# At each seam between two stages, two of eight input blocks are multiplied early, as an old and a new term

## The chip, the cores and the metric

The kernel runs on one core of a Trainium2 chip. The metric is the device time of one execution in microseconds (us), the median of several runs; lower is better.

## The reference

A stream of 272 tokens (16 meta tokens and 256 of the sequence) with 1024 features goes through two layers, and its last 256 tokens through a third. Every layer is a chain of stages of one form, "multiply the normed stream by weights, norm the result, add it to the stream":

```python
for i in range(DEPTH):
    g = norm_g[i]
    f1 = swiglu(rmsnorm(h, g[0]), ffn_w_gate[i, 0], ffn_w_up[i, 0], ffn_w_down[i, 0])
    h = h + FFN_RES * rmsnorm(f1, g[1])
    hn = rmsnorm(h, g[2])
    m = neighborhood_attention(hn, ...) if i % N_MIXERS == 0 else diff_attention(hn, ...)
    h = h + rmsnorm(m, g[3])
    f2 = swiglu(rmsnorm(h, g[4]), ffn_w_gate[i, 1], ffn_w_up[i, 1], ffn_w_down[i, 1])
    h = h + FFN_RES * rmsnorm(f2, g[5])
...
x = x + rms_norm(mixed @ w_out, g_mix_post)      # hybrid layer: its input is rms_norm(x, g_mix_pre) @ w_in
u = jnp.square(jax.nn.relu(rms_norm(x, g_mlp_pre) @ w_up))
x = x + rms_norm(u @ w_down, g_mlp_post)
```

`rmsnorm(x, g)` is `x * rsqrt(mean(x*x) + 1e-6) * g`, the mean over the 1024 features of a token. All of it is float32.

## The kernel before

**Layout.** The stream `h` lies transposed in SBUF: eight blocks of 128 features (the partitions), each 272 tokens wide (256 once the meta tokens are no longer needed). A product is a matmul with a 128x128 piece of weight as the stationary operand and one block of the input as the moving one, summed over the eight input blocks in one PSUM tile. There are six such PSUM tiles (`ps_mm`, 128 x 272 each) and two small ones (`ps_t`).

**Precision.** Each float32 operand is split in two float32r parts, a high one and the rest, and three products are summed: high x high, high x low, low x high. For the input these parts are the tiles `xh` and `xl`, for the weights `wh` and `wl`. Weights arrive by DMA, ACT makes `wh` (line 156), DVE makes `wl` (line 168), and up to seven pairs are held; `W.pump` hands out this work between the products.

**A seam.** There are seven places where one stage ends and the next begins, here called seams: after a down projection of a feed-forward stage (four times; three of them 272 columns wide, the fourth, ahead of the hybrid layer, 256 wide), and after an output projection of attention (three times; 272, 256 and 256 columns wide). At a seam this happens:

1. `Post.evac(ps, j)` takes the eight output blocks of the ending stage as they are finished: ACT squares a block (line 387, or 385 in two halves for the last), DVE adds the square to `accf` (line 388), and ACT writes the block times its gain into `f` (line 603). For the last block, PE first sums `accf` over the partitions ("row sums", line 344), then the squares `sq` of the last block.
2. `Post.finish`: DVE makes the mean of both sums (lines 356, 362), POOL raises it to -1/2 (line 349), and PE spreads the result over the partitions in a PSUM tile, `post.bc` (lines 368 to 373). Meanwhile PE runs nine matmuls whose result nobody reads (`turn_over`, line 476), and nine more behind the spreading.
3. DVE makes `f*bc` (`addend`, line 617, tile `hb`), and from it for blocks 0 and 1 the new `xh` at once (line 486); for blocks 2 to 7 it adds `hb` to `h` (line 623) and ACT makes `xh` (line 436). PE starts on each block as its `xh` comes: four output tiles, `wh` and `wl`, that is eight matmuls for each block (lines 502, 503), 64 in all. DVE then makes the eight `xl` (line 453), and PE does 32 matmuls with these (line 506).
4. The norm of the new stream is not in `xh`: it is a factor for each token, `rb`, which is applied to the products. Its squares are made by ACT (line 495) and summed by DVE in three additions, the last of them into `accp` (lines 447 to 449, `Norm.sum`). `Norm.head` makes PE's row sums of `accp` a part of the next product (the fifth output tile): it stands behind that tile's twelfth matmul. `Norm.tail` spreads `rb`.

The order on each engine is the order of the program text; the tile framework sets the semaphores between engines, and it also lets no two engines touch one PSUM tile at the same time.

Of the kernel before, what the change touches and what calls it, by code (L numbers as in the profile page):

```python
# [10 lines left out]
F32 = mybir.dt.float32  # L11
# [10 lines left out]
T = S + NM  # L22
# [13 lines left out]
R_BUFS = 3  # L36

# [172 lines left out]
def block_kernel(ctx: ExitStack, tc: tile.TileContext, a, out):  # L210
# [13 lines left out]
    def nm(s):  # L224
        uid[0] += 1
        return f"{s}_{uid[0]}"
# [196 lines left out]
    class Norm:  # L423


        def __init__(self, g, cols):
            self.g, self.cols = g, cols
            self.xh = bp.tile([128, 8, T], FR, name=nm("xh"), tag="xh", bufs=1)
            self.xl = bp.tile([128, 8, T], FR, name=nm("xl"), tag="xl", bufs=1)
            self.x = (self.xh, self.xl)  # L430
            self.acc = tp.tile([128, T], F32, name=nm("accp"), tag="acc", bufs=1)
            self.first, self.second = {3: self.head}, {1: self.tail}
# [5 lines left out]
        def square(self, j):  # L438
            c = self.cols
            q = square_into(self.acc, h[:, j, c], j, c, engine=pool)  # L440
            if q is not None:
                pool.tensor_tensor(self.acc[:, c], self.acc[:, c], q[:, c], op=OP.add)

        def sum(self, sq):

            c = self.cols
            dve.tensor_tensor(sq[:, 0:4, c], sq[:, 0:4, c], sq[:, 4:8, c], op=OP.add)
            dve.tensor_tensor(sq[:, 0:2, c], sq[:, 0:2, c], sq[:, 2:4, c], op=OP.add)
            dve.tensor_tensor(self.acc[:, c], sq[:, 0, c], sq[:, 1, c], op=OP.add)

# [14 lines left out]
    def start_phase(norm, post, n=4):  # L465
# [22 lines left out]
        for k in range(2, 8):  # L488
# [5 lines left out]
        for x, y in ((2, 6), (6, 8), (0, 2)):  # L494
            act.activation(squares[:, x:y, c], h[:, x:y, c], AF.Square)
            if x:
                W.high()
        for k in range(8):
            norm.low(k)
        for k in range(8):  # L500
            for q in range(n):
                pe.matmul(ps[q][:, c], w[q][0][:, k, :], norm.xh[:, k, c], start=k == 0, stop=False)  # L502
                pe.matmul(ps[q][:, c], w[q][1][:, k, :], norm.xh[:, k, c], start=False, stop=False)  # L503
        for k in range(8):
            for q in range(n):
                pe.matmul(ps[q][:, c], w[q][0][:, k, :], norm.xl[:, k, c], start=False, stop=k == 7)  # L506
        W.low_if()
        norm.sum(squares)
        W.done(n)
        return ps  # L510
# [78 lines left out]
    class Post:  # L589


        def __init__(self, g, cols, bias=None, gbias=None):
            self.g, self.cols, self.bias, self.gbias = g, cols, bias, gbias
# [15 lines left out]
        def finish(self, between=lambda n: None):  # L609
            r = rstd_head(self.m, self.cols, self.sq)  # L610
            between(9)
            self.bc = rstd_tail(r, self.cols)
# [279 lines left out]
    post = Post(half_gains(0, 1), ALL)  # L892
# [42 lines left out]
    norm = Norm(gains(0, 2), ALL)  # L935
# [218 lines left out]
    post = Post(gains(0, 3), ALL, vgain("b_o"), gbo)  # L1154
# [3 lines left out]
    norm = Norm(gains(0, 4), ALL)  # L1158
    post2 = Post(half_gains(0, 5), ALL)
# [14 lines left out]
    norm = Norm(gains(1, 0), ALL)  # L1174
    post = Post(half_gains(1, 1), ALL)
# [3 lines left out]
    norm = Norm(gains(1, 2), ALL)  # L1179
# [115 lines left out]
    post = Post(gains(1, 3), GRID)  # L1295
    proj_out(post, (Oh, Ol))

    norm = Norm(gains(1, 4), GRID)
    post2 = Post(half_gains(1, 5), GRID)
# [3 lines left out]
    norm = Norm(vgain("mix_pre"), GRID)  # L1303
# [17 lines left out]
    pg, *ps4 = start_phase(norm, post2)  # L1321
# [275 lines left out]
    post = Post(vgain("mix_post"), GRID)  # L1597
# [3 lines left out]
    norm = Norm(vgain("mlp_pre"), GRID)  # L1601
# [120 lines left out]
```

## Time and profile before

| | |
|---|---|
| median of 3 runs | 1429.81 us (1429.76 to 1431.71) |
| the profiled execution | 1431.22 us |
| its span, first to last instruction | 1429.4 us |
| mean granted TensorE clock | 0.998 |
| PE busy | 1408.2 us, 99% of the span |
| DVE busy | 893.7 us, 63% |
| ACT busy | 750.2 us, 52% |

A share of busy time is a mean over the whole span; at a seam the engines stand otherwise. Times in the trace are microseconds from the start of the span. PE's weight loads have rows of their own (PEld) and run ahead of the matmul that they belong to.

### The profile page before, as it was taken

How to read it: one execution, taken by the hardware profiler on the slowest of the kernel's cores; microseconds unless marked ns; L12 is line 12 of the kernel's file. 1: busy time of each engine (PE TensorE's matmuls, PEld its weight loads, DVE VectorE, ACT ScalarE, POOL GpSimd, SP SyncE). 2: the span in 40 equal slices, each digit the busy share in tenths (PEclk: the TensorE clock that was granted, in tenths of full speed). 3: DMA queues.
4: the chain of work that ended last, by engine and by line, in shares of the span. 5: the costliest groups of instructions: out<-in, count | busy, mean ns of one | idle time of the engine just before them, and what ended most of it. 6: DMA issues, size and time to landing. Idle time of an engine off the chain costs nothing.

```text
span 1429.4 us, 26895 instructions
## 1 busy us (share of the span) xinstructions
PE 1408.2 (99%) x11068; PEld 1357.6 (95%) x11068; DVE 893.7 (63%) x1668; ACT 750.2 (52%) x1333; POOL 168.1 (12%) x185
## 2 busy tenths in 40 slices
PE   9999999999999999999999999999999999999997
PEld 9999999899999999999999888999999888899886
DVE  6776447664865544955546785776555877686542
ACT  5554346666554444644445564664444565676441
POOL 1325001010221200212100001031100000000000
PEclk9999999999999999999999999999999999999999
DMA  7875552352575554555553352375554543275650
GB/s 250 271 251 172 179 185 66 124 167 90 167 229 172 168 180 148 175 180 177 163 182 99 119 177 89 112 244 184 188 178 131 177 129 108 89 234 179 221 177 30
DMA packets 219528, 234.41 MB, mean 164 GB/s; under 512 B 5313, under 2 KB 209894, under 8 KB 219214
## 3 DMA queue, kind: packets, MB, share of 16 engines
q1 hardware_dynamic: 218206, 227.38, 49.2%
q0 software_dynamic: 656, 4.94, 1.1%
q8 instruction: 87, 1.43, 0.4%
q10 hardware_dynamic: 544, 0.38, 0.1%
q14 instruction: 35, 0.29, 0.1%
HBM read 231.62 MB, written 5.13 MB: 166 GB/s over the span
## 4 chain that ended last, share of the span: by engine, by line
PE 91%; DVE 6%; ACT 2%; DMA 1%; issue 1%; POOL 0%; DVEq 0%; POOLq 0%; ACTq 0%; SPq 0%
PE pm L393 24%; PE pm L395 24%; PE pm L394 23%; PE ps L1645 2%; PE ps L1644 2%; PE ps L1646 2%; PE pm L506 2%; DVE wl L168 2%; PE pm L502 2%; PE pm L503 1%; DMA wr<-in_da_w_qkv_dram 1%; PE pt L344 1%; PE pt L1013 1%; PE pm L540 1%; PE ps L1022 1%
## 5 line engine op out<-in xcount | busy, mean ns | idle before, releaser
L168 DVE TENSOR_TENSOR wl<-wr,wh 128x1024 fp32r<-128x1024 f32 (+1 forms) x430 | 514.3, 1204 | 122.9 <-ACT wh L156 122.2
L393 PE MATMUL pm<-xh,wh 128*128 128x272 f32 (+1 forms) x1992 | 581.4, 292 | 2.2 <-DVE Ol L421 2.2
L395 PE MATMUL pm<-xh,wl 128*128 128x272 f32 (+1 forms) x1992 | 570.4, 286 | 0.0
L394 PE MATMUL pm<-xl,wh 128*128 128x272 f32 (+1 forms) x1992 | 568.5, 285 | 0.0
L156 ACT ACTIVATE wh<-wr 128x1024 fp32r<-128x1024 f32 (+1 forms) x430 | 440.7, 1033 | 194.0 <-PE pm L394 112.9
L393 PEld LDWEIGHTS pm<-xh,wh 128*128 128x128 f32 x1992 | 376.0, 189 | 11.2 <-issue 9.4
L395 PEld LDWEIGHTS pm<-xh,wl 128*128 128x128 f32 x1992 | 375.9, 189 | 0.1
L394 PEld LDWEIGHTS pm<-xl,wh 128*128 128x128 f32 x1992 | 375.6, 189 | 0.1
L395 PE MATMUL pm<-mh,wl 128*128 128x272 f32 (+1 forms) x704 | 202.2, 287 | 0.0
L393 PE MATMUL pm<-mh,wh 128*128 128x272 f32 (+1 forms) x704 | 202.1, 287 | 0.0
L394 PE MATMUL pm<-ml,wh 128*128 128x272 f32 (+1 forms) x704 | 201.5, 286 | 0.0
L650 POOL TENSOR_TENSOR sr<-sl,rb 128x272 f32<-128x272 f32 (+1 forms) x88 | 104.5, 1192 | 320.1 <-ACT sl L648 320.1
L395 PEld LDWEIGHTS pm<-mh,wl 128*128 128x128 f32 x704 | 132.7, 188 | 0.0
L394 PEld LDWEIGHTS pm<-ml,wh 128*128 128x128 f32 x704 | 132.6, 188 | 0.0
L393 PEld LDWEIGHTS pm<-mh,wh 128*128 128x128 f32 x704 | 132.6, 188 | 0.0
L420 ACT ACTIVATE mh<-m 128x272 fp32r<-128x272 f32 (+1 forms) x88 | 37.7, 428 | 117.8 <-DVE m L655 117.6
L655 DVE TENSOR_TENSOR m<-pm,sr 128x272 f32<-128x272 f32 (+1 forms) x88 | 38.3, 435 | 80.5 <-PE pm L395 74.8
L648 ACT ACTIVATE sl<-gq 128x272 f32<-128x272 f32 (+1 forms) x88 | 36.9, 427 | 95.8 <-DVE gq L646 95.6
L349 POOL TENSOR_TENSOR s<-s,mhalf 128x3 f32<-128x3 f32 (+1 forms) x15 | 19.1, 1274 | 558.4 <-DVE s L362 336.1
L646 DVE TENSOR_TENSOR gq<-pm,rb 128x272 f32<-128x272 f32 (+1 forms) x88 | 37.6, 435 | 71.6 <-PE pm L395 69.0
L388 DVE TENSOR_TENSOR accf<-accf,sq 128x272 f32<-128x272 f32 (+1 forms) x42 | 18.3, 436 | 81.9 <-ACT sq L387 81.8
L502 PE MATMUL pm<-xh,wh 128*128 128x272 f32 (+1 forms) x224 | 56.7, 291 | 0.6
(337 smaller groups left out, 1728.6 us busy)
## 6 DMA issues: line engine op xcount, KB each, us to landing
wr<-in_ffn_w_gate_dram SPq DMA_DIRECT2D x43, 1024.0 KB
wr<-in_ffn_w_up_dram SPq DMA_DIRECT2D x43, 1024.0 KB
wr<-in_ffn_w_down_dram SPq DMA_DIRECT2D x32, 1024.0 KB
wr<-in_w_up_dram SPq DMA_DIRECT2D x16, 1024.0 KB
wr<-in_w_down_dram SPq DMA_DIRECT2D x16, 1024.0 KB
wr<-in_ffn_w_down_dram SPq DMA_DIRECT2D x16, 768.0 KB
wr<-in_na_w_qkv_dram SPq DMA_DIRECT2D x12, 1024.0 KB
wr<-in_da_w_qkv_dram SPq DMA_DIRECT2D x12, 1024.0 KB
```

Source lines behind the costliest of these rows:

```text
L156: self.nc.scalar.activation(hi, w, AF.Copy)
L168: engine.tensor_tensor(lo, w, hi.bitcast(F32), op=OP.subtract)
L393: pe.matmul(ps, wh[:, k, :], xh[:, j, cols], start=start, stop=False)
L394: pe.matmul(ps, wh[:, k, :], xl[:, j, cols], start=False, stop=False)
L395: pe.matmul(ps, wl[:, k, :], xh[:, j, cols], start=False, stop=stop)
L420: act.activation(hi, src, AF.Copy)
L502: pe.matmul(ps[q][:, c], w[q][0][:, k, :], norm.xh[:, k, c], start=k == 0, stop=False)
L506: pe.matmul(ps[q][:, c], w[q][0][:, k, :], norm.xl[:, k, c], start=False, stop=k == 7)
L646: dve.tensor_tensor(t[:, c], ps[:, c], norm.rb[:, c], op=OP.mult)
L648: act.activation(s[:, c], t[:, c], AF.Silu)
L650: pool.tensor_tensor(s2[:, c], s[:, c], norm.rb[:, c], op=OP.mult)
L655: dve.tensor_tensor(t[:, c], ps[:, c], gated.pop(f)[:, c], op=OP.mult)
```

## The change

For input blocks 2 and 3 and two of the four first output tiles, the new stream `h + f*bc` is no longer waited for. While the ending stage is still finishing, `Norm.ahead` (called in `evac` for output blocks 5 and 6) splits `g*h` and `g*f` of these two blocks into high and low parts, in places 4 to 7 of `xh` and `xl`, which are free at that time. `start_phase` multiplies both with the weights: 12 matmuls with the old stream go into the output tiles themselves, 12 with `f` into two further PSUM tiles, `term`. These 24 take the place of the 18 matmuls of `turn_over`. When `bc` is there, ACT copies it into SBUF, DVE makes `term*bc` (tile `fs`) between the fourth and the fifth `xl`, and when the tile is complete DVE adds both into an SBUF tile `fb`, from which the next step reads. The 12 matmuls of these blocks and tiles in the main loops are gone, and blocks 2 and 3 come last there.

The core of the diff:

```diff
+AHEAD = (2, 3)
+ORDER = (0, 1, 4, 5, 6, 7, 2, 3)
...
+        def ahead(self, i, f):
+            c, j = self.cols, AHEAD[i]
+            for n, src in ((4 + i, h), (6 + i, f)):
+                act.activation(self.xh[:, n, c], src[:, j, c], AF.Copy, scale=self.g[:, j:j + 1])
+                dve.scalar_tensor_tensor(self.xl[:, n, c], src[:, j, c], self.g[:, j:j + 1],
+                                         self.xh[:, n, c].bitcast(F32), op0=OP.mult, op1=OP.subtract)
...
-        def turn_over(m):
-            x = w[0][0].rearrange("p a b -> p (a b)")[:, 0:256]
+        term = {q: ps_mm() for q in early}
+
+        def products():
+            for x, into in ((4, {q: ps[q] for q in early}), (6, term)):
+                for i in range(2):
+                    k = AHEAD[i]
+                    for q in early:
+                        for part, v in ((0, norm.xh), (1, norm.xh), (0, norm.xl)):
+                            last = x == 6 and i == 1 and part == 0 and v is norm.xl
+                            pe.matmul(into[q][:, c], w[q][part][:, k, :], v[:, x + i, c],
+                                      start=i == 0 and part == 0 and v is norm.xh, stop=last)
+                            yield
+        todo = products()
+        def some(m):
             for _ in range(m):
-                pe.matmul(ps[0][:, 0:256], x[:, 0:128], x, start=True, stop=True)
-
+                next(todo, None)
+        some(3)
         old = [tmp("go") for _ in range(2)]
         for k in range(2):
             act.activation(old[k][:, c], h[:, k, c], AF.Copy, scale=norm.g[:, k:k + 1])
-        post.finish(turn_over)
-        turn_over(9)
+        post.finish(lambda: some(11 if c is ALL else 10))
+        some(24)
+        bc = tmp("bc")
+        act.activation(bc[:, c], post.bc[:, c], AF.Copy)
...
+        scaled = {}
+        for i, k in enumerate(ORDER):
+            norm.low(k)
+            if i == 3:
+                for q in early:
+                    scaled[q] = tmp("fs")
+                    dve.tensor_tensor(scaled[q][:, c], term[q][:, c], bc[:, c], op=OP.mult)
...
         W.low_if()
         norm.sum(squares)
+        for q in early:
+            x = tmp("fb")
+            dve.tensor_tensor(x[:, c], scaled[q][:, c], ps[q][:, c], op=OP.add)
+            ps[q] = x
...
         def evac(self, ps, j):
             c = self.cols
+            if j == 4:
+                self.norm = Norm(self.gain, c)
+            if j in (5, 6):
+                self.norm.ahead(j - 5, self.f)
             if j == NB - 1:
                 self.m = mean_head(self.acc, c)
```

Three places show what this does to the order on the engines. On PE, at the first seam, behind the last matmul of the down projection, stood the row sums of `accf` and of `sq` (tiles `pt`), the nine idle-filling matmuls, and the spreading of the factor `s` with `ident`:

```order
L344 MATMUL pt_2563<-ones,accf_126 128x1 x3
L344 MATMUL pt_2588<-ones,sq_2569 128x1 x3
L476 MATMUL pm_2580<-wh_2402 128x256 x9
L368 MATMUL pt_2605<-ident,s_2594 128x128
L369 MATMUL pt_2605<-ident,s_2594 128x128
L370 MATMUL pt_2605<-ident,s_2594 128x16
```

Now three early products stand between the two groups of row sums, and eleven behind them:

```order
L346 MATMUL pt_2573<-ones,accf_125 128x1 x3
L487 MATMUL pm_2587<-xh_2369,wh_2408 128x272
L487 MATMUL pm_2587<-xh_2369,wl_2409 128x272
L487 MATMUL pm_2587<-xl_2370,wh_2408 128x272
L346 MATMUL pt_2600<-ones,sq_2579 128x1 x3
L487 MATMUL pm_2588<-xh_2369,wh_2438 128x272
L487 MATMUL pm_2588<-xh_2369,wl_2439 128x272
L487 MATMUL pm_2588<-xl_2370,wh_2438 128x272
```

On DVE, at the same seam, the mean (`s`) and the first `hb`, which reads `post.bc` (`pt`), stood like this, with the engine that each waits for:

```order
L356 TENSOR_SCALAR s_2564<-pt_2563 128x3 [waits PE_49]
L362 SCALAR_TENSOR_TENSOR s_2589<-pt_2588,s_2564 128x3 [waits DVE_49,PE_49]
L617 TENSOR_TENSOR hb_2618<-f_125,pt_2605 128x272 [waits PE_49]
L486 SCALAR_TENSOR_TENSOR xh_2573<-hb_2618,G,go_2584 128x272 [waits DVE_49,Activation_49]
L617 TENSOR_TENSOR hb_2621<-f_125,pt_2605 128x272
```

Now the first `hb` waits for ACT (`Activation`), whose one instruction at this place that touches the same PSUM tile is the copy of `bc`:

```order
L358 TENSOR_SCALAR s_2574<-pt_2573 128x3 [waits PE_49]
L364 SCALAR_TENSOR_TENSOR s_2601<-pt_2600,s_2574 128x3 [waits DVE_49,PE_49]
L655 TENSOR_TENSOR hb_2635<-f_124,pt_2619 128x272 [waits Activation_49]
L508 SCALAR_TENSOR_TENSOR xh_2369<-hb_2635,G,go_2596 128x272 [waits DVE_49]
L655 TENSOR_TENSOR hb_2638<-f_124,pt_2619 128x272
```

On DVE, ahead of the seam behind the first output projection, the last three additions of squares into `accf` (output blocks 4, 5 and 6) stood between pairs of weight splits:

```order
L388 TENSOR_TENSOR accf_4123<-accf_4123,sq_4354 128x272
L168 TENSOR_TENSOR wl_4324<-wr_3953,wh_4323 128x1024
L168 TENSOR_TENSOR wl_4327<-wr_3953,wh_4326 128x1024
L388 TENSOR_TENSOR accf_4123<-accf_4123,sq_4393 128x272
L168 TENSOR_TENSOR wl_4360<-wr_4110,wh_4359 128x1024
L168 TENSOR_TENSOR wl_4366<-wr_4110,wh_4365 128x1024
L388 TENSOR_TENSOR accf_4123<-accf_4123,sq_4429 128x272
L356 TENSOR_SCALAR s_4459<-pt_4458 128x3
```

Now two `xl` of `ahead` stand ahead of the second and two ahead of the third of these additions:

```order
L390 TENSOR_TENSOR accf_4137<-accf_4137,sq_4370 128x272
L170 TENSOR_TENSOR wl_4338<-wr_3967,wh_4337 128x1024
L170 TENSOR_TENSOR wl_4341<-wr_3967,wh_4340 128x1024
L453 SCALAR_TENSOR_TENSOR xl_4369<-h,G,xh_4368 128x272
L453 SCALAR_TENSOR_TENSOR xl_4369<-f_4136,G,xh_4368 128x272
L390 TENSOR_TENSOR accf_4137<-accf_4137,sq_4413 128x272
L170 TENSOR_TENSOR wl_4376<-wr_4124,wh_4375 128x1024
L170 TENSOR_TENSOR wl_4382<-wr_4124,wh_4381 128x1024
L453 SCALAR_TENSOR_TENSOR xl_4369<-h,G,xh_4368 128x272
L453 SCALAR_TENSOR_TENSOR xl_4369<-f_4136,G,xh_4368 128x272
L390 TENSOR_TENSOR accf_4137<-accf_4137,sq_4453 128x272
L358 TENSOR_SCALAR s_4483<-pt_4482 128x3
```

## Rows read from the trace of the kernel before

**Rows 1.** The page: busy time and share of the span by engine.

```profile
PE 1408.2 (99%) x11068; PEld 1357.6 (95%) x11068; DVE 893.7 (63%) x1668; ACT 750.2 (52%) x1333; POOL 168.1 (12%) x185
```

**Rows 2.** Timeline, first seam, 272 columns: start, length, engine, line, operation, count.

```profile
213.93 0.76 PEld L344 LDWEIGHTS pt<-ones,accf 128*128 128x128 f32 x6
214.61 0.75 PEld L344 LDWEIGHTS pt<-ones,sq 128*128 128x128 f32 x6
216.66 0.13 PEld L368 LDWEIGHTS pt<-ident,s 128*128 128x128 f32 x1 [0.24 <-POOL s L349]
...
217.26 0.44 DVE L617 TENSOR_TENSOR hb<-f,pt 128x272 f32<-128x272 f32 x1 [1.62 <-PE pt L370]
...
224.85 3.39 DVE L453 SCALAR_TENSOR_TENSOR xl<-h,G,xh 128x272 fp32r<-128x272 f32 x8
...
231.37 0.45 DVE L449 TENSOR_TENSOR accp<-f 128x272 f32<-128x272 f32 x1
...
232.19 0.76 PEld L344 LDWEIGHTS pt<-ones,accp 128*128 128x128 f32 x6
```

**Rows 3.** Timeline, runs of equal instructions: matmuls of both widths, DVE reading PSUM.

```profile
226.82 4.15 PE L506 MATMUL pm<-xl,wh 128*128 128x272 f32 x32
...
1110.54 3.90 PE L506 MATMUL pm<-xl,wh 128*128 128x256 f32 x32
...
236.23 0.79 DVE L949 TENSOR_TENSOR qkv<-pm,rb 128x272 f32<-128x272 f32 x2 [1.86 <-ACT rb L462]
...
1255.99 0.76 DVE L1608 SCALAR_TENSOR_TENSOR rl<-pm,rb 128x256 f32<-128x256 f32 x2 [0.44 <-ACT rb L462]
```

**Rows 4.** Groups by line: busy, mean ns | idle before it, what ended it.

```profile
L462 ACT ACTIVATE rb<-pt 128x272 f32<-128x272 f32 (+1 forms) x8 | 3.1, 393 | 24.1 <-PE pt L370 16.6 <-PE pt L373 7.6
...
L1484 DVE TENSOR_TENSOR rx<-pm,sg 128x256 f32<-128x256 f32 x8 | 3.4, 420 | 3.2 <-ACT raw L1482 3.2
```

**Rows 5.** Timeline, 256-column seam behind the last feed-forward down projection.

```profile
1098.68 0.53 PEld L344 LDWEIGHTS pt<-ones,accf 128*128 128x128 f32 x4
1099.33 0.52 PEld L344 LDWEIGHTS pt<-ones,sq 128*128 128x128 f32 x4
...
1114.99 0.42 DVE L449 TENSOR_TENSOR accp<-f 128x256 f32<-128x256 f32 x1
...
1115.54 0.53 PEld L344 LDWEIGHTS pt<-ones,accp 128*128 128x128 f32 x4
```

**Rows 6.** Timeline, the three seams behind output projections: last addition, row sums.

```profile
357.03 0.44 DVE L388 TENSOR_TENSOR accf<-accf,sq 128x272 f32<-128x272 f32 x1
...
357.67 0.76 PEld L344 LDWEIGHTS pt<-ones,accf 128*128 128x128 f32 x6
358.41 0.79 PEld L344 LDWEIGHTS pt<-ones,sq 128*128 128x128 f32 x6
...
905.81 0.43 DVE L388 TENSOR_TENSOR accf<-accf,sq 128x256 f32<-128x256 f32 x1 [0.28 <-ACT sq L387]
...
906.53 0.53 PEld L344 LDWEIGHTS pt<-ones,accf 128*128 128x128 f32 x4
907.18 0.52 PEld L344 LDWEIGHTS pt<-ones,sq 128*128 128x128 f32 x4
...
1235.18 0.43 DVE L388 TENSOR_TENSOR accf<-accf,sq 128x256 f32<-128x256 f32 x1 [0.57 <-ACT sq L387]
...
1235.66 0.52 PEld L344 LDWEIGHTS pt<-ones,accf 128*128 128x128 f32 x4
...
1236.25 0.52 PEld L344 LDWEIGHTS pt<-ones,sq 128*128 128x128 f32 x4
```

**Rows 7.** PE's longest waits (timeline), and a stretch behind one (the 0.50 is the granted clock).

```profile
270.61 0.19 PEld L393 LDWEIGHTS pm<-xh,wh 128*128 128x128 f32 x1 [2.27 <-issue]
...
888.04 0.14 PEld L1259 LDWEIGHTS pt<-ident,keep 128*128 128x128 f32 x1 [1.53 <-DVE keep L1253]
...
272.00:275.40 3.40, 3.40 (x19) 3.29 (x16) 0.72 (x4) 0.90 (x3) 0.00 (x0) 0.50 0.61 206
```

More of the change, by code (lines that the diff above doesn't have):

```diff
@@ L430, in __init__ @@
             self.x = (self.xh, self.xl)
-            self.acc = tp.tile([128, T], F32, name=nm("accp"), tag="acc", bufs=1)
             self.first, self.second = {3: self.head}, {1: self.tail}
@@ L436, in block @@
             act.activation(self.xh[:, j, c], h[:, j, c], AF.Copy, scale=self.g[:, j:j + 1])
[L438 to L442, printed above, removed]
         def sum(self, sq):
             c = self.cols
+            self.acc = tp.tile([128, T], F32, name=nm("accp"), tag="acc", bufs=1)
             dve.tensor_tensor(sq[:, 0:4, c], sq[:, 0:4, c], sq[:, 4:8, c], op=OP.add)
@@ L463, in tail, with start_phase @@
             return self.rb
-    def start_phase(norm, post, n=4):
+    def start_phase(norm, post, n=4, early=(0, 1)):
         c = norm.cols
@@ L487, in start_phase @@
                                      op0=OP.mult, op1=OP.add)
-        for k in range(2, 8):
+        for k in ORDER[2:]:
             post.block(k)
@@ L497, in start_phase @@
                 W.high()
[L498 to L502, printed above, removed]
+        tiles = {k: [q for q in range(n) if k not in AHEAD or q not in early] for k in ORDER}
+        for k in ORDER:
+            for q in tiles[k]:
+                pe.matmul(ps[q][:, c], w[q][0][:, k, :], norm.xh[:, k, c], start=k == 0 and q not in early, stop=False)
                 pe.matmul(ps[q][:, c], w[q][1][:, k, :], norm.xh[:, k, c], start=False, stop=False)
-        for k in range(8):
-            for q in range(n):
-                pe.matmul(ps[q][:, c], w[q][0][:, k, :], norm.xl[:, k, c], start=False, stop=k == 7)
+        for k in ORDER:
+            for q in tiles[k]:
+                last = max(ORDER.index(x) for x in ORDER if q in tiles[x])
+                pe.matmul(ps[q][:, c], w[q][0][:, k, :], norm.xl[:, k, c], start=False, stop=k == ORDER[last])
         W.low_if()
         norm.sum(squares)
+        for q in early:
+            x = tmp("fb")
+            dve.tensor_tensor(x[:, c], scaled[q][:, c], ps[q][:, c], op=OP.add)
+            ps[q] = x
         W.done(n)
@@ L607, in evac, with finish @@
                                bias=self.gbias[:, j:j + 1])
-        def finish(self, between=lambda n: None):
+        def finish(self, between):
             r = rstd_head(self.m, self.cols, self.sq)
-            between(9)
+            between()
             self.bc = rstd_tail(r, self.cols)
@@ L890, in prepare @@
         yield
-    post = Post(half_gains(0, 1), ALL)
+    post = Post(half_gains(0, 1), ALL, gains(0, 2))
     bg_list.append(prepare())
@@ L932, in block_kernel @@
     QT = [slice(NM, NM + 128), slice(NM + 128, T)]
-    norm = Norm(gains(0, 2), ALL)
+    norm = post.norm
     kq = slot(5, F32, "kq")
@@ L1153, in block_kernel @@
     mixer(norm, post, na_evac, na_attention, ALL, na_before)
-    post = Post(gains(0, 3), ALL, vgain("b_o"), gbo)
+    post = Post(gains(0, 3), ALL, gains(0, 4), vgain("b_o"), gbo)
     proj_out(post, (Oh, Ol))
-    norm = Norm(gains(0, 4), ALL)
-    post2 = Post(half_gains(0, 5), ALL)
+    norm = post.norm
+    post2 = Post(half_gains(0, 5), ALL, gains(1, 0))
     t5b = []
@@ L1173, in block_kernel @@
     ffn(norm, post2, post)
-    norm = Norm(gains(1, 0), ALL)
-    post = Post(half_gains(1, 1), ALL)
+    norm = post2.norm
+    post = Post(half_gains(1, 1), ALL, gains(1, 2))
     ffn(norm, post, post2)
-    norm = Norm(gains(1, 2), ALL)
+    norm = post.norm
     kq = slot(5, F32, "kq")
@@ L1294, in block_kernel @@
     mixer(norm, post, da_evac, da_attention, GRID, lambda n: None)
-    post = Post(gains(1, 3), GRID)
+    post = Post(gains(1, 3), GRID, gains(1, 4))
     proj_out(post, (Oh, Ol))
-    norm = Norm(gains(1, 4), GRID)
-    post2 = Post(half_gains(1, 5), GRID)
+    norm = post.norm
+    post2 = Post(half_gains(1, 5), GRID, vgain("mix_pre"))
     ffn(norm, post2, post)
-    norm = Norm(vgain("mix_pre"), GRID)
+    norm = post2.norm
     Oh, Ol = slot(0, FR, "Oh"), slot(1, FR, "Ol")
@@ L1320, in block_kernel @@
     act.preload_act_table_set("natural_log_exp_and_others")
-    pg, *ps4 = start_phase(norm, post2)
+    pg, *ps4 = start_phase(norm, post2, early=(1, 2))
     gi = cp.tile([128, 2, 36], F32, name="gi")
@@ L1596, in block_kernel @@
         bg()
-    post = Post(vgain("mix_post"), GRID)
+    post = Post(vgain("mix_post"), GRID, vgain("mlp_pre"))
     proj_out(post, (Oh, Ol), [4, 5, 6, 7, 0, 1, 2, 3])
-    norm = Norm(vgain("mlp_pre"), GRID)
+    norm = post.norm
     before = post
```

6 lines of the change are left out of this document (3 added, 3 removed).

## Prediction

> **What bounds the kernel now.** I began with the busy shares. PE works through 99% of the span, so the first thought is that matmuls are what costs time, and that 12 fewer of them behind each norm are a gain [rows 1]. But that share is a mean over stages, so I read the timeline of one seam engine by engine, and followed what PE waits for there.
>
> At the first seam PE's last weight load for a product of the old stage is followed at 213.93 by the row sums of `accf`, at 214.61 by those of `sq`, with no pause between them (six loads, 0.68 us, 0.114 us each). At 216.66 the spreading of the factor begins, 0.24 us after the last of the filling matmuls, on the word of POOL. At 217.26 DVE makes the first `hb`, and from then until 231.82, the end of `accp`, DVE works without a pause worth the name: `hb`, `xh`, `h`, then eight `xl` from 224.85 (3.39 us), a weight split, and the three sums. PE's row sums of `accp` are loaded at 232.19, that is 0.37 us behind the end of `accp` [rows 2]. The shortest hand-over from DVE to these row sums that I find is 0.05 us (an addition ends at 1235.61, its row sums are loaded at 1235.66) [rows 6]. So at a 272-column seam DVE's chain has 0.32 us to spare before PE has to stand still, although PE is the busy engine. At the last feed-forward seam, 256 columns wide, `accp` ends at 1115.41 and the load comes at 1115.54: 0.08 us to spare [rows 5]. The two engines are as good as tied there. Behind these row sums the next product, the factor `rb` and everything else follow in PE's order. The seam is over when both the products before this point and DVE's chain have come to it, so what counts is not the number of matmuls but the later of the two.
>
> **The change, part by part.** Durations of runs of equal instructions give the step from one to the next: matmuls of 272 columns (4.15-0.29)/31 = 0.125 us, of 256 columns 0.117 us; DVE operations that read PSUM 0.36 us (272) and 0.34 us (256) [rows 3]; `xl` (3.39-0.49)/7 = 0.41 us [rows 2].
>
> *What PE saves.* Twelve matmuls per seam after the norm: 12 x 0.125 = 1.5 us at four seams, 12 x 0.117 = 1.4 us at three, 10.2 us in all. The 24 early ones lie in the waits of the norm, where the 18 filling ones were. Eleven of them take 1.38 us where nine and 0.24 us of waiting stood: no cost that I can see, at most 0.1 us a seam. But this saving only brings PE sooner to row sums that wait for DVE.
>
> *Three early products ahead of the row sums of `sq`.* These sums start the chain to `bc`. At 272 columns PE went from one group of row sums to the other without a pause, so 3 x 0.125 = 0.37 us go straight into the chain. At 256 columns 0.65 us lay between the loads where four loads take 0.46 us [rows 5], so of 3 x 0.117 = 0.35 us some 0.16 us remain.
>
> *The copy of `bc`.* DVE's first `hb` now waits for ACT, not for PE. Is this wait real? The kernel has a place of that kind already: `rx` reads a PSUM tile that ACT copies just before it, and takes nothing from the copy. Yet it stood idle 3.2 us in all until ACT's copy (line 1482) had ended [rows 4]. The price is the nearest row: ACT's copy of the like tile into `rb` takes 0.39 us, so 0.40 us with the hand-over, at each seam. The Trainium skill (PSUM — Partial Sum Buffer, "PSUM bank collisions raise a hardware error") says that two engines, even two readers, must not be in one bank at once and that the hardware doesn't make one wait, so the program has to; a reader who trusted parallel reads would leave this term out, and come to 9.0 us where the sum below comes to 11.8. The row of `rx` is on the side of the wait. Lower bound of the term: nothing; upper: 0.45 us.
>
> *Two `term*bc` in DVE's chain*, between the `xl` and so ahead of `accp`: 2 x 0.36 = 0.72 us, or 0.68 us. Lower bound: there is none but this, since DVE has no pause to take them. The two additions into `fb` stand behind `accp`, while DVE waits for the row sums (0.7 us) anyway; no cost, or 0.1 us if they run over.
>
> *The work of `ahead`.* Two ACT and two DVE operations at output blocks 5 and 6. In the feed-forward down projections DVE and ACT have more than a microsecond free for each block, so this is hidden. Behind the output projections it is not. There DVE's last addition to `accf` ends 0.20 us ahead of its row sums (357.47 to 357.67), 0.29 us (906.24 to 906.53) and 0.05 us (1235.61 to 1235.66); ahead of it DVE idles only for 0 us, 0.28 us and 0.57 us [rows 6]. Four `xl` are 1.65 us of DVE. Less these margins (each end-to-load time less the 0.05 us of hand-over) the row sums come later by 1.65-0.15 = 1.50, of which I take 1.40 because smaller gaps close up too; 1.65-0.28-0.24 = 1.13; and 1.65-0.57 = 1.08 us. The three early products behind them then cost: 0.68+0.375 us where 0.74 us stood between the two loads, so 0.32 us; 0.46+0.35 where 0.65 and 0.59 us stood, so 0.16 and 0.22 us. Nothing is queued ahead that could make up for it: `sq` is ready by then, and all that follows waits for these sums. Lower bound: half, if the weight splits before them can slide; upper: the full 1.65 us.
>
> *The sum*, each with its spare time taken off:
> - three 272-column feed-forward seams: 0.37+0.40+0.72-0.32 = 1.17 us each, 3.5 us;
> - the 256-column one: 0.16+0.40+0.68-0.08 = 1.16 us;
> - first output projection: 1.40+0.32+0.40+0.72-0.32 = 2.5 us;
> - second and third: 1.13+0.16+0.40+0.68-0.08 = 2.3 us, and 1.08+0.22+1.00 = 2.3 us.
>
> That is 11.8 us (11.7 to 11.9 by rounding). The profiled execution, 1431.22 us, would become 1443.0; it lies 1.4 us above the median of the three runs, so for the median I forecast 1429.8+11.8 = 1441.6 us.
>
> At the row sums of `accp` PE then stands still: the 1.5 us that it saved, plus 1.17 us of lateness less the 0.8 us by which its own start is late, about 1.8 us at each seam.
>
> **Rivals.**
> - *The clock falls in these new waits.* After its longest wait, 2.27 us at 270.61, PE ran from 272.0 to 275.4 at a granted 0.50, that is 1.2 GHz; after one of 1.53 us at 888.04 it did not [rows 7]. The new waits of about 1.8 us, with row sums of one column behind them, lie between the two. Each fall would cost up to 3.4/2 = 1.7 us, less what still waits, say 1.4. Three of the ten new waits: 1446 us; six: 1450. The Trainium skill (TensorE: Matmul & The Clock Gate, "HAM oscillation — how this bites in real kernels") describes such falls from waits between bursts of matmuls.
> - *A smaller loss.* The wait for `bc` is hidden, or the output projections lose half: 11.8-2.8-1.6 = 7.4 us, 1437 us.
> - *The count of matmuls decides, and it is faster.* Then `accp` must be ready when PE comes to it, and the chain no later than before: 10.2 us less about 2 us for the three early products, 1421.6 us. For it speaks PE's 99%; against it, that DVE would have to end `accp` about 1.8 us sooner than I expect, and it has 0.32 and 0.08 us to spare now. Below a lateness of DVE's chain equal to 0.32 us there is a gain, above it none.
> - *No change* (within 0.2%, 2.9 us, about what a measurement of this kernel can tell): the loss at the output projections is met by gains at the others. About 1430 us.
>
> **How the numbers follow.** The sum as it stands, with at most one fall of the clock, 0.52; several falls 0.26; the smaller loss 0.12; no change 0.05; faster 0.05. The range from 1436 to 1448 us holds the first, the third and the smaller part of the second. Faster 0.05, same 0.05, slower 0.90.
>
> **What would show it.** In the new profile: DVE's first `hb` released by ACT, about 0.40 us behind the spreading; the row sums of `sq` 0.4 us later behind those of `accf`; row sums of `accf` waiting for DVE at the three output projections, by 1.0 to 1.5 us; and PE's row sums of `accp` waiting for DVE at all seven seams, 1.7 to 1.9 us each. If PE does not wait at `accp`, I am wrong in the main point; if it waits much less, DVE's chain has a pause that I overlooked; a granted clock under 1 behind these waits is the first rival.

## The result: 0.9% slower, as forecast, and the profile after

The changed kernel takes 1443.56 us (median of 4 runs, 1442.73 to 1444.87) where the kernel before takes 1430.62 us (4 runs); the ratio is 1.0091, with a 95% interval from 1.0073 to 1.0108. The forecast was 1441.6 us, in a range from 1436 to 1448.

The page's first row of the profile after shows less PE work and more DVE and ACT work than [rows 1], which by itself would speak for a gain:

```profile
PE 1406.1 (98%) x11026; PEld 1353.4 (94%) x11026; DVE 914.2 (63%) x1724; ACT 763.1 (53%) x1368; POOL 169.9 (12%) x185
```

The timeline of the first seam after, rows of PE, PEld, DVE and ACT put in order of time (start, length, engine, line, operation; in brackets the idle time before it and what ended it), answers to [rows 2]:

```profile
213.09 0.76 PEld L346 LDWEIGHTS pt<-ones,accf 128*128 128x128 f32 x6
214.14 0.76 PEld L346 LDWEIGHTS pt<-ones,sq 128*128 128x128 f32 x6
...
216.87 0.40 ACT L504 ACTIVATE bc<-pt 128x272 f32<-128x272 f32 x1 [1.80 <-PE pt L372]
217.30 0.44 DVE L655 TENSOR_TENSOR hb<-f,pt 128x272 f32<-128x272 f32 x1 [2.11 <-ACT bc L504]
...
224.72 1.74 DVE L458 SCALAR_TENSOR_TENSOR xl<-h,G,xh 128x272 fp32r<-128x272 f32 x4
226.37 0.78 DVE L522 TENSOR_TENSOR fs<-pm,bc 128x272 f32<-128x272 f32 x2
227.07 1.73 DVE L458 SCALAR_TENSOR_TENSOR xl<-h,G,xh 128x272 fp32r<-128x272 f32 x4
228.72 1.22 DVE L170 TENSOR_TENSOR wl<-wr,wh 128x1024 fp32r<-128x1024 f32 x1
...
229.99 0.19 PEld L397 LDWEIGHTS pm<-xh,wl 128*128 128x128 f32 x1 [0.51 <-DVE wl L170]
...
231.93 0.44 DVE L445 TENSOR_TENSOR accp<-f 128x272 f32<-128x272 f32 x1
...
232.52 0.80 PE L346 MATMUL pt<-ones,accp 128*128 128x1 f32 x6 [1.00 <-DVE accp L445]
```

The row sums of `sq` start 1.05 us behind those of `accf`, where it was 0.68 us. ACT copies `bc`, and DVE's first `hb` comes 0.03 us behind the end of that copy. The two `fs` stand in the middle of the `xl`. PE then waits twice for DVE, once for the weight split `wl` and once for `accp`. That this is no matter of one seam shows in the groups of waits (engine, line, waited for, total us, times, longest); none of these groups has a counterpart before:

```profile
PE pt L346 <- DVE accp L445: 6.9, 7, 1.0
PE pt L346 <- DVE accf L390: 2.9, 3, 1.1
PE pm L397 <- DVE wl L170: 2.4, 7, 0.4
```

The granted clock of stretches behind these waits (window, its length, busy time and count of PE, PEld, DVE, ACT and POOL, then the granted clock, DMA share and GB/s):

```profile
233.00:237.00 4.00, 4.00 (x21) 4.00 (x22) 1.37 (x3) 0.00 (x0) 1.76 (x1) 0.57 0.26 64
...
274.00:278.00 4.00, 4.00 (x37) 3.83 (x35) 2.00 (x5) 2.21 (x6) 0.00 (x0) 1.00 0.49 164
...
1124.00:1128.00 4.00, 4.00 (x23) 4.00 (x23) 2.65 (x4) 0.00 (x0) 1.61 (x1) 0.57 0.54 177
```

Behind the waits for `accp` at the first and the sixth seam the clock fell to the lower level, 1.2 GHz, for a little over 3 us each. The fall of before at 272 [rows 7] isn't there at the same place, though the wait in front of it is as long.

To see where the 12.0 us between the two spans (1429.4 and 1441.4) lie, I took the start of the same matmul in both timelines and followed the difference:

| stretch | difference, us | forecast, us |
|---|---|---|
| first 9 us, waits for the input's DMA (the first seam's start lies from -1.7 to +0.7 us in the other profiles) | -0.8 | none |
| row sums of `accf` to row sums of `accp`, seven seams | +1.03, 1.02, 1.10, 1.09, 1.12, 1.32, 1.19: 7.9 | 8.2 |
| row sums of `accf` late at the three output projections | +1.27, 0.98, 1.14: 3.4 | 3.6 |
| falls of the clock behind seams 1 and 6 | +1.59, +1.62: 3.2 | at most one |
| the fall of before at 272 that is gone | -1.5 | none |
| all the rest | -0.2 | none |

(The lines are rounded one by one.)

### The profile page after: what moved, and what is told of

Read it like the earlier page. It is cut to its first block, busy times and chain, and to the rows that moved or that the text cites. A ratio compares the mean times of both kernels' runs of the same rounds, so it can differ in the third digit from the quotient of the medians.

```text
span 1441.4 us, 26917 instructions
## 1 busy us (share of the span) xinstructions
PE 1406.1 (98%) x11026; PEld 1353.4 (94%) x11026; DVE 914.2 (63%) x1724; ACT 763.1 (53%) x1368; POOL 169.9 (12%) x185
## 4 chain that ended last, share of the span: by engine, by line
PE 83%; DVE 12%; ACT 3%; DMA 1%; issue 1%; POOL 0%; POOLq 0%; DVEq 0%; SPq 0%; ACTq 0%
PE pm L395 23%; PE pm L397 22%; PE pm L396 22%; DVE wl L170 3%; PE ps L1683 2%; PE ps L1682 2%; PE ps L1684 2%; DVE xl L458 2%; DVE hb L655 1%; DVE h L661 1%; PE pt L346 1%; PE pm L487 1%; PE ps L1278 1%; ACT wh L158 1%; DVE f L443 1%
## 5 line engine op out<-in xcount | busy, mean ns | idle before, releaser
L395 PE MATMUL pm<-xh,wh 128*128 128x272 f32 (+1 forms) x1992 | 582.8, 293 | 2.2 <-DVE Ol L423 2.2
L395 PE MATMUL pm<-Oh,wh 128*128 128x256 f32 (+1 forms) x192 | 56.5, 294 | 0.5 <-ACT Oh L422 0.5
```

The costliest lines, as they stand in the source:

```text
L395: pe.matmul(ps, wh[:, k, :], xh[:, j, cols], start=start, stop=False)
```

## Experiments

Two measures are used. The time is a median, and the kernel before in the same series stands beside it: 1429.94 us for the first four kernels, 1430.26 for the next four, 1431.07 for e9 to e11 and 1431.82 for e12. The second measure doesn't depend on the clock elsewhere: the time from PE's first row sum of `accf` to that of `accp`, read from each timeline. For all kernels but e8, which has no `accp` (us; a star marks a fall of the clock between the two):

| kernel | seam 1 | 2 | 3 | 4 | 5 | 6 | 7 |
|---|---|---|---|---|---|---|---|
| before | 18.27 | 18.39 | 18.22 | 18.22 | 16.88 | 16.86 | 16.81 |
| changed | 19.30 | 19.41 | 19.32 | 19.31 | 18.00 | 18.18 | 18.00 |
| e1 | 18.61 | 20.27* | 18.62 | 18.61 | 17.33 | 17.50 | 17.33 |
| e2 | 19.01 | 21.43* | 19.01 | 19.02 | 17.72 | 17.62 | 17.74 |
| e3 | 18.92 | 20.58* | 18.92 | 18.93 | 17.65 | 18.18 | 17.66 |
| e4 | 19.30 | 19.40 | 19.31 | 19.31 | 17.99 | 18.17 | 17.99 |
| e5, on before | 17.90 | 18.01 | 17.85 | 17.84 | 16.82 | 16.75 | 16.77 |
| e6, on before | 18.59 | 18.71 | 18.53 | 18.55 | 17.38 | 17.42 | 17.35 |
| e7 | 17.93 | 18.06 | 17.94 | 17.95 | 16.71 | 17.14 | 16.71 |
| e9, on e7 | 18.97 | 19.06 | 18.97 | 18.96 | 17.70 | 17.78 | 17.70 |
| e10, on before | 19.46 | 19.60 | 19.45 | 19.45 | 17.99 | 17.92 | 17.87 |
| e11 | 19.31 | 19.42 | 19.32 | 19.31 | 17.99 | 18.18 | 19.56* |
| e12, on e7 | 17.74 | 18.05 | 17.75 | 17.75 | 16.71 | 16.66 | 16.72 |

**e1: `fs` behind `accp`.**

```diff
+        for q in early:
+            kept[q] = tmp("fs")
+            act.activation(kept[q][:, c], term[q][:, c], AF.Copy)
...
-                    dve.tensor_tensor(scaled[q][:, c], term[q][:, c], bc[:, c], op=OP.mult)
...
         norm.sum(squares)
+        for q in early:
+            scaled[q] = kept[q]
+            dve.tensor_tensor(scaled[q][:, c], kept[q][:, c], bc[:, c], op=OP.mult)
```

> ACT copies both term tiles into SBUF right behind its copy of bc, where it is idle for almost 3 us, and DVE's two term*bc move behind accp. Theory (the seam ends with DVE's chain): accp ends 0.72 us sooner at four seams and 0.68 at three, PE's wait in front of its row sums shrinks by as much, and the time falls from 1443.6 by 4.9 us to about 1438.7; a fall of the clock that goes away with the shorter wait would add up to 1.6 us to that. Rival (PE's own work, the split products and their order, is what costs): PE's work is the same, so the time stays within 1 us of 1443.6.

Measured: 1441.71 us, 1.9 us less than the changed kernel, not 4.9. The four runs lie far apart, from 1438.89 us at a mean granted clock of 0.999 to 1443.12 at 0.994, so the time alone decides little. The seams became shorter by 0.67 to 0.70 us, all that was expected. But part of it was given back at once, and the DVE rows of the third seam show how:

```profile
586.25 0.44 DVE L445 TENSOR_TENSOR accp<-f 128x272 f32<-128x272 f32 x1
586.61 0.79 DVE L540 TENSOR_TENSOR fs<-fs,bc 128x272 f32<-128x272 f32 x2
587.31 0.78 DVE L543 TENSOR_TENSOR fb<-fs,pm 128x272 f32<-128x272 f32 x2
588.01 0.15 DVE L358 TENSOR_SCALAR s<-pt 128x3 f32<-128x3 f32 x1
```

The mean `s`, which starts the chain to `rb`, now stands behind four operations and waits for DVE (no idle time in front of it), so that ACT's `rb` at that seam comes 22.43 us behind the row sums of `accf`, 0.44 us sooner than in the changed kernel instead of 0.70. A step that is moved off one chain must not be put ahead of the next one.

**e2: the copy of `bc` behind the last `xh`.**

```diff
-        bc = tmp("bc")
-        act.activation(bc[:, c], post.bc[:, c], AF.Copy)
...
             post.block(k)
             norm.block(k)
+        bc = tmp("bc")
+        act.activation(bc[:, c], post.bc[:, c], AF.Copy)
```

> ACT copies bc behind the last xh instead of ahead of DVE's first hb. Theory: the first hb comes 0.40 us sooner behind the spreading at all seven seams, and all behind it too, 2.8 us in all: about 1440.8. Rival (two readers of one PSUM tile don't hinder each other, and the wait in the trace is something else): the first hb starts 0.4 us behind the spreading as before, and the time stays within 1 us of 1443.6. If the copy now delays ACT's squares, the first addition of the squares would wait for ACT; I expect it not to, as a weight split ends later than they do.

Measured: 1444.08 us (1441.30 to 1445.05), no gain in time. In the timeline, at the six seams without a fall of the clock, DVE's first `hb` comes 0.41 to 0.45 us sooner behind the row sums of `accf` (0.69 at the sixth), and the row sums of `accp` 0.26 to 0.31 us sooner (0.56 at the sixth): the wait was real. The time shows nothing of it; in the profile the clock took it back:

```profile
361.00:368.00 7.00, 7.00 (x35) 7.00 (x34) 1.93 (x6) 0.11 (x1) 0.86 (x1) 0.52 0.35 120
...
795.00:801.00 6.00, 6.00 (x28) 6.00 (x29) 1.77 (x4) 0.91 (x2) 1.76 (x1) 0.50 0.53 171
```

These two falls are twice as long as the others. All four runs had a mean granted clock of 0.993 to 0.995, where the changed kernel had 0.997 in three of four; 0.003 of 1440 us is 4 us.

**e3: no early products between the row sums.**

```diff
-        some(3)
         old = [tmp("go") for _ in range(2)]
```

> The three early products between the row sums of accf and of sq go behind the row sums of sq; the 24 are all still there. Theory: the mean, the factor and bc come sooner by 0.37 us at the four seams of 272 columns, and by 0.16 to 0.22 us at the three of 256 columns, 2.0 us in all: about 1441.6. Rival (the three only fill time that is waited through anyway): no difference beyond 1 us.

Measured: 1442.38 us (1440.98 to 1443.29), 1.2 us less. The table gives 0.38 to 0.40 us at the three 272-column seams without a fall, 0.35 and 0.34 at the fifth and seventh, nothing at the sixth. There `bc` doesn't wait for PE. ACT loads a table (`ACT_TABLE_LOAD`) ahead of `go` and of the copy, as these rows of the changed kernel show:

```profile
1106.56 1.28 ACT L1358 ACT_TABLE_LOAD   x1
1107.85 0.91 ACT L500 ACTIVATE go<-h,V 128x256 f32<-128x256 f32 x2
1108.67 0.36 ACT L504 ACTIVATE bc<-pt 128x256 f32<-128x256 f32 x1
```

The copy follows on `go` without a pause, so sooner row sums bring nothing at this seam, and e2, which takes the copy out of this queue, gains more there than elsewhere.

**e4: the splits at the output projections earlier.**

```diff
+            if j == 4 and self.proj:
+                for i in range(2):
+                    self.norm.ahead(i, self.f, (1,))
...
+        post.proj = True
+        post.norm = Norm(post.gain, c)
+        for i in range(2):
+            post.norm.ahead(i, None, (0,))
```

> At the three output projections only, the split of h is made ahead of the projection and the split of f at output block 4, where DVE waited 0.97 us for ACT in the third projection. Theory (DVE's sum of squares is late for the row sums of accf there): these row sums come sooner by some 1.2 us at the first, 0.6 at the second and 1.1 us at the third projection, so 2.9 us in all: about 1440.7. Rival (what is late there is the product of the projection, so that PE waits for weights): under 1 us of difference.

Measured: 1443.44 us (1441.66 to 1448.07), no gain. The row sums of `accf` were late by 0.42, 0.28 and 0.18 us instead of 1.27, 0.98 and 1.14, so the splits at blocks 5 and 6 were what had made them late. But PE's work ahead of and in the projections now came 1.3, 0.6 and 1.2 us later, because I had put the split of `h` (the second edit; the first is that of `f`) in front of what attention still had to do:

```profile
1216.14 0.89 ACT L452 ACTIVATE xh<-h,V 128x256 fp32r<-128x256 f32 x2
1216.94 0.36 ACT L422 ACTIVATE Oh<-ps 128x256 fp32r<-128x256 f32 x1
...
1216.67 0.89 DVE L453 SCALAR_TENSOR_TENSOR xl<-h,V,xh 128x256 fp32r<-128x256 f32 x2 [1.28 <-ACT xh L452]
```

At the third projection DVE stood idle 1.28 us for the split's `xh`, with work of attention queued behind. The cost was moved, not removed.

**e5: the matmuls alone, on the kernel before.**

```diff
         for k in range(8):
-            for q in range(n):
+            for q in range(2 if k in (2, 3) else 0, n):
```

> The kernel before, without the 12 matmuls of input blocks 2 and 3 into the first two output tiles at each seam; this leaves out part of the products, and nothing else changes. Theory (PE is ahead of DVE's chain by 0.32 us at four seams and 0.08 us at three, and no more): the time falls by these alone, 1.5 us, to about 1428.4, and PE waits some 1.2 us in front of the row sums of accp at every seam. Rival (the number of matmuls decides): 12 x 0.125 at four seams and 12 x 0.117 us at three, 10.2 us, to about 1419.7.

Measured: 1428.04 us (11 runs) against 1430.26, ratio 0.9985 (0.9977 to 0.9994). Twelve matmuls fewer per seam, 10.2 us of PE's work, are worth 2.2 us; the seams became shorter by 0.37 to 0.38 us at 272 columns and by 0.04 to 0.11 at 256. The rival in which the count decides is out. PE's wait in front of `accp` was 0.29 us at 272 columns and 0.55 at 256, not the 1.2 us that I had expected: at the first seam some 0.5 us of the 1.5 us that PE saved went into waits for the next `xh` before that.

**e6: the two DVE products alone, on the kernel before.**

```diff
             norm.low(k)
+            if k == 3:
+                for q in range(2):
+                    x = tmp("fs")
+                    dve.tensor_tensor(x[:, c], post.bc[:, c], t[q][:, c], op=OP.mult)
```

> The kernel before, with two more products of DVE (a tile in SBUF times post.bc, whose result nobody reads) between the fourth and the fifth xl; PE's work is that of before. Theory: 0.72 us less 0.32 us at the four seams of 272 columns and 0.68 less 0.08 us at the three of 256, so 4 x 0.40 + 3 x 0.60 = 3.4 us, to about 1433.3, and up to 1.6 us more for a fall of the clock. Rival (DVE's work is hidden behind PE, which is busy 99% of the time): no difference.

Measured: 1433.70 us (9 runs) against 1430.26, ratio 1.0026 (1.0016 to 1.0035), so 3.4 us. The seams: 0.31 to 0.33 us more at 272 columns, 0.50 to 0.56 at 256. Of 0.72 us the first 0.40, and of 0.68 us the first 0.12 to 0.18, are swallowed by DVE's spare time; the rest comes through. In the profile the seven seams add up to 2.9 us, so the 3.4 us are not the seams' alone: at the second output projection the row sums of `accf` came 1.05 us later as well, as ACT stood idle 2.67 us for the DMA of a weight there, 1.35 us before.

**e7: all four costs out of the way.** e2 and e3, the copies of e1 but with `fs` and `fb` behind the spreading of `rb`, and at the projections the split of `h` at block 0, that of `f` at block 4.

```diff
+        def late():
+            for x, y, p in terms:
+                dve.tensor_tensor(y[:, c], y[:, c], bc[:, c], op=OP.mult)
+                dve.tensor_tensor(x[:, c], y[:, c], p[:, c], op=OP.add)
+        norm.late = late
...
             act.activation(self.rb[:, self.cols], p[:, self.cols], AF.Copy)
+            self.late()
```

> The changed kernel with all the suspected costs taken out of the way: both terms are copied to SBUF by ACT and multiplied by bc behind the spreading of rb, bc is copied behind the last xh, the three early products go behind the row sums of sq, and at the output projections the split of h is made at block 0 and that of f at block 4. Theory: DVE's chain from the factor to accp is that of before, and PE comes to its end 1.5 us early; so it gains the 0.32 and 0.08 us that PE was behind, 1.5 us in all, less some 0.9 us that remain of the split of f at the projections, less one or two more falls of the clock (1.6 us each) in PE's waits of 1.2 us: about 1431, between 1428 and 1433, no real difference to before. Rival (something else in the change costs, such as the early products or the new order of the blocks): it stays above 1438.

Measured: 1430.69 us (12 runs) against 1430.26, ratio 1.0005 (0.9997 to 1.0013). All of the loss is gone. By time alone the single steps don't add up to this: e1 to e4 are faster than the changed kernel by 1.9, -0.5, 1.2 and 0.1 us, e7 by some 12.5. e1 and e4 moved their cost to another place, which e7 avoids, and their mean clock and that of e2 and e3 was 0.993 to 0.997 in all runs but one, 0.996 to 0.999 in e7. In the seams they do add up. At the third seam the three steps in the seam add up: 0.70 (e1), 0.31 (e2) and 0.40 (e3) make 1.41 us, and e7 is 1.38 us shorter than the changed kernel. PE still waits 0.9 to 1.0 us for `accp` at each seam: what is left of the idea is PE's spare time, with nothing to spend it on. The group of these waits in e7 (total us, times, longest):

```profile
PE pt L346 <- DVE accp L446: 6.5, 7, 1.0
```

**e8: PE sums four blocks instead of DVE.**

```diff
-            dve.tensor_tensor(sq[:, 0:2, c], sq[:, 0:2, c], sq[:, 2:4, c], op=OP.add)
-            dve.tensor_tensor(self.acc[:, c], sq[:, 0, c], sq[:, 1, c], op=OP.add)
...
-            self.r = rsqrt(mean_head(self.acc, self.cols), 2 if self.cols is GRID else 3)
+            self.r = rsqrt(mean_head([self.sq[:, k] for k in range(4)], self.cols), 2 if self.cols is GRID else 3)
```

> The one before, and DVE no longer makes the second and third addition of the squares (0.73 and 0.44 us); PE sums four blocks over the partitions instead of one, 9 more one-column matmuls at 272 columns (1.03 us) and 6 more at 256 (0.69 us). Theory: DVE's chain ends 1.16 us sooner, where PE now stands in wait; PE's own work grows by 1.03 and 0.69 us of the 1.5 and 1.4 us that it saves; so 0.5 us of gain at four seams and 0.7 at three, 4.1 us, less the 0.9 us at the projections, and no new fall of the clock, as the wait is gone: about 1426.7. Rival (PE's wait isn't for DVE): slower than the one before by up to 6 us, the time of the added matmuls.

Measured: 1440.83 us (6 runs) against 1430.26: a miss of 14 us. PE's row at the second seam tells why:

```profile
374.79 2.73 PE L348 MATMUL pt<-ones,f 128*128 128x1 f32 x24
```

There is no wait in front of it, so the mechanism holds, but I had mispriced it. The program's three row sums are six matmuls in the trace, as [rows 2] shows with x6; twelve are 24. PE's added work is 18 x 0.114 = 2.05 us, not 1.03, which is more than the 1.5 us it had saved; from row sums of `accf` to ACT's `rb` a 272-column seam without a fall takes 22.4 us, and 21.5 to 21.6 in e7. A part of the miss is again the clock: three of the six runs had a mean of 0.992 and took 1443.6 to 1443.7 us, the others 0.998 and 1436.2 to 1438.0.

**e9 and e10: two additions of `h` on POOL, on e7 and on the kernel before.**

```diff
+        for k in range(2):
+            pool.tensor_tensor(h[:, k, c], h[:, k, c], t[k][:, c], op=OP.add)
...
-        for k in range(2):
-            dve.tensor_tensor(h[:, k, c], h[:, k, c], t[k][:, c], op=OP.add)
```

> The kernel with all four costs out of the way (e7), and POOL instead of DVE makes the two additions of h for blocks 0 and 1, right behind their xh; DVE's chain loses 0.79 us. Theory (that chain sets the end of the seam, and PE waits about 1 us for it): 0.79 us less at all seven seams, 5.5 us, less what POOL's use of SBUF slows DVE: from 1430.7 to about 1425.2, between 1424 and 1428, which is faster than before by 0.15 to 0.45%. Rival (PE is the bound once the four costs are gone): no difference to 1430.7.

> The kernel before, with the same move to POOL and nothing else. Theory: there PE is behind DVE by 0.32 and 0.08 us already, so a shorter chain of DVE gains nothing: no difference to before beyond 1 us, and accp ends 0.79 us sooner at each seam without PE's row sums coming sooner. Rival (DVE alone is the bound of the seam): 5.5 us faster.

Measured: 1438.55 and 1440.58 us against 1431.07. Both expectations fell, by the same cause, seen in the rows of POOL and DVE at the first seam of e10:

```profile
216.44 0.76 POOL L489 TENSOR_TENSOR h<-h,hb 128x272 f32<-128x272 f32 x1 [1.24 <-DVE hb L617]
...
216.40 1.09 DVE L486 SCALAR_TENSOR_TENSOR xh<-hb,G,go 128x272 fp32r<-128x272 f32 x1
217.42 0.42 DVE L617 TENSOR_TENSOR hb<-f,pt 128x272 f32<-128x272 f32 x1
217.96 1.10 DVE L486 SCALAR_TENSOR_TENSOR xh<-hb,G,go 128x272 fp32r<-128x272 f32 x1
```

The same operation in the kernel before:

```profile
217.81 0.50 DVE L486 SCALAR_TENSOR_TENSOR xh<-hb,G,go 128x272 fp32r<-128x272 f32 x1
```

DVE's `xh` takes 1.09 us beside POOL's addition, and 0.50 us without it. PE waits for just these two `xh`, so each seam starts 1.2 us later: the table's row of e10 is 1.2 us above before at 272 columns and 1.1 at 256, 8.1 us in all. These two runs test nothing about the bound, then; that test is e12.

**e11: the waits for `accp` filled.**

```diff
         def head(self):
+            if self.fill:
+                p = ps_t()
+                for _ in range(8):
+                    pe.matmul(p[:, 0:256], self.xh[:, 0, 16:144], self.xh[:, 0, 16:272], start=True, stop=True)
```

> The changed kernel, with eight matmuls of 256 columns, whose result nobody reads, in front of the row sums of accp, about 0.9 us of the 1.0 to 1.2 us that PE waits there. Theory that falls of the clock behind these waits are part of the loss (two in the profile, some 1.6 us each): no granted clock under 1 within 4 us of the row sums of accp, and 1.5 to 3.5 us less than the changed kernel, 1440 to 1442. Rival (the falls behind the row sums don't come from these waits): falls there as before, and the same time, 1443.6, or a little more.

Measured: 1448.21 us (1445.69 to 1450.79) against 1431.07: more, not less. In the profile no fall follows the row sums of `accp` any more; one stands at 272, as before, and one at the last seam behind the row sums of `accf`:

```profile
376.00:384.00 8.00, 7.62 (x61) 7.22 (x60) 6.93 (x11) 2.51 (x4) 1.70 (x1) 1.00 0.12 30
...
1248.00:1251.60 3.60, 3.60 (x19) 3.60 (x19) 0.32 (x2) 0.66 (x2) 0.70 (x1) 0.53 0.58 203
```

The profiled run, with a mean clock of 0.996, has two falls, as many as the changed kernel, at other places; the other three runs had 0.992 to 0.994, less than any run of the changed kernel. So the falls came elsewhere, and not fewer. The row sums of `accf` were also 0.84 and 0.78 us later at the second and third projection than in the changed kernel. These rows of ACT show what held them up:

```profile
910.99 1.06 ACT L158 ACTIVATE wh<-wr 128x1024 fp32r<-128x1024 f32 x1 [1.75 <-DMA wr<-in_ffn_w_gate_dram]
...
1244.68 1.06 ACT L158 ACTIVATE wh<-wr 128x1024 fp32r<-128x1024 f32 x1 [1.93 <-DMA wr<-in_w_up_dram]
```

ACT waited for the DMA of a weight, 0.61 and 1.15 us in the changed kernel, with the last `xh` of `ahead` behind it in its queue. Why the weight came later is not shown. This is 1.6 us of the profiled run's loss that has nothing to do with the clock, so e11 is no clean test of what the falls cost.

**e12: DVE's chain shortened, on e7.**

```diff
                     if not (last and m2 == 3):
                         W.pump()
+                    elif q == 0:
+                        post.split = W.n_split < W.n_high
+                        W.low_if()
...
-        W.low_if()
+        if not post.split:
+            W.low_if()
         norm.sum(squares)
```

> The kernel with all four costs out of the way (e7), and at the four feed-forward seams DVE makes the weight split that stands between the xl and the squares (1.22 us) ahead of the seam, behind the sum of output block 6, where it waited 1.96 us for PE. Theory (DVE's chain sets the end of the seam, and PE waits about 1.2 us for it): the row sums of accp come 1.1 to 1.2 us sooner at four of seven seams, 4.4 to 4.9 us in all, to about 1426, 0.3% faster than before, and PE's wait there is gone. Rival (PE is the bound once the four costs are gone): no difference to 1430.7. If the split makes the row sums of accf late, they show a wait for DVE at the feed-forward seams, and up to 1 us a seam is lost again.

Measured: 1429.56 us (11 runs) against 1431.82, ratio 0.9984 (0.9975 to 0.9993). This version beats both kernels, the one before by 0.16% and the changed one by some 1%; the gain on the kernel before is half of what was expected. The rows of DVE and ACT at the first seam show the next in line:

```profile
226.98 0.64 ACT L524 ACTIVATE f<-h 128x544 f32<-128x544 f32 x1
...
227.66 1.29 DVE L444 TENSOR_TENSOR f<-f 128x1088 f32<-128x1088 f32 x1 [0.85 <-ACT f L524]
```

DVE comes to the squares 1.22 us sooner and then waits 0.85 us for ACT's last one, at all four seams where the split was moved (3.5 us in the group of waits). ACT makes two weight splits between its three squares. By the table that leaves 0.2 us at the first, third and fourth seam and 0.5 at the sixth, 1.1 us; the rest of the difference between the ratios of e7 and e12 lies within their intervals.

## Why the prediction was right, point by point

*The seam ends with DVE's chain, not with the count of matmuls.* Shown, from both sides: e5 takes 10.2 us of PE's work away and gains 2.2 us, e6 adds 5 us to DVE's chain, nothing to PE, and loses 3.4 us. The spare time that I read from the rows, 0.32 and 0.08 us, is what e5 got back (0.37 and 0.04 to 0.11) and, a little larger, what e6 had to use up (0.72 less 0.32, and 0.68 less 0.50 to 0.56).

*The copy of `bc`.* Taken as 0.40 us; e2 brings the first `hb` 0.41 to 0.45 us sooner at five of six seams. At the other, the sixth, I had overlooked ACT's queue: the copy stands behind the 1.28 us of the table, and that seam lost 1.32 us instead of 1.16. The Trainium skill (PSUM — Partial Sum Buffer, "PSUM bank collisions raise a hardware error") has it that even two readers of one bank must be kept apart by the program; the trace agrees as to the wait, 0.40 us of copy and 0.03 us of hand-over. Of this 0.3 us reached the row sums of `accp` at most seams. The rest was met by something that I had overlooked: in the changed kernel the first two `xh` start 0.03 us behind their `hb`, in the kernel before and in e2 0.10 to 0.11 us behind.

*The three early products* were 0.37 and some 0.16 to 0.22 us; e3 gives 0.39 and 0.35, 0, 0.34, so this term was 0.1 to 0.2 us too small at the fifth and seventh seam. It didn't show in the sum, as those two `xh` gave back some 0.15 us at each seam. *The two `fs`* were 0.72 and 0.68; e1 gives 0.70 and 0.67. *The two `fb`* cost nothing, as said: they end before `s` starts.

*The work of `ahead` at the projections*: 1.40, 1.13 and 1.08 us were taken, 1.27, 0.98 and 1.14 came. e4 shows that it is the splits, and that this work is not free a few microseconds earlier either.

*PE's new wait.* I had 1.7 to 1.9 us in front of the row sums of `accp`. It is 1.7 us, from where PE would be (1.53 us early) to where it is (0.20 us late), but in two parts: 0.5 us for the weight split `wl`, which stands behind `fs` in DVE's queue and which I had overlooked as an operand of the next product, and 1.2 us for `accp`.

*The clock, and luck.* Of the 2.0 us between 1441.6 and 1443.56, 0.8 us is the base: the forecast added its sum to 1429.8, and the median of all four runs of the kernel before is 1430.6. The sum itself, 11.8 us, meets the 12.0 us of the profile (12.9 by the medians) more closely than its terms do: the seams and projections came to 0.5 us less than forecast and the start to 0.8 us less, while the clock took 1.7 us more, as two falls behind the new waits (3.2 us) replaced the one at 272 (1.5 us). That these offset each other is luck. A smaller slip: half of the 3.6 us at the output projections is 1.8 us, not the 1.6 us of the rival with a smaller loss. That waits for row sums are part of the cause of the falls is not shown by an experiment; it rests on their places and on the mean clock, 0.995 to 0.997 in the changed kernel and 0.999 in nine of the twelve runs of e7. In the 14 profiles the clock fell 19 times before the last 10 us: 7 times behind the wait near 270, 11 times behind row sums of `accf` or `accp` for which PE had waited 0.97 to 1.77 us, and once, in e8, behind 24 row sums without a wait. What decides which wait is followed by a fall stays open: e7 keeps a wait of 0.9 to 1.0 us at each `accp` and has no fall there in its profile, and filling them (e11) didn't help.

## What to carry to other kernels

Where two engines end a stage nearly together, read the spare time between them, from the end of the one to the load of the other, before work is taken from either; here some 0.3 us was all that 1.5 us fewer matmuls could earn, and whatever the edit put on the other engine beyond that counted. An edit that frees one engine needs a partner that shortens the other's chain: neither e5's saving nor e7 gave much alone, and with e12 the two together gave a small gain, 0.16%, until the third engine, ACT, was in line. Work moved off a chain lands in some queue, so look at what stands behind it there: the mean `s` in e1, the attention in e4, the two `xh` in e10.

## What the runs showed of the hardware

A DVE operation with two inputs in SBUF took 1.09 us instead of 0.50 us while POOL added two SBUF tiles for 0.76 us (e10, 14 of 14 such operations between 1.04 and 1.11 us; in e9 between 1.05 and 1.11). The Trainium skill (SBUF — State Buffer, "SBUF: two separate sides") says that DVE and POOL share a pair of ports that one of them holds for a whole instruction; the trace agrees in that one of the two is held up, and the price is 0.6 us of DVE for 0.76 us of POOL. Which of the two had the ports first the rows don't show: DVE's operation, the one that is held up, starts 0.04 us before POOL's, by times that are rough for POOL.

The same wait need not give the same clock. The wait of 2.2 us near 270 is there in all 14 profiles; in 7 of them the granted clock fell behind it, in 7 it did not. In two of the latter, the changed kernel and e4, it had fallen at 233, behind the first seam; in the other five it had not. So a single profile doesn't tell what falls of the clock an edit will cost.
